# Two loads in another order, and a spacer of 32 bytes in place of 224, in a hybrid streaming encoder step

## The chip, the cores and the metric

The kernel runs on one core of one Trainium2 chip. The metric is the time of one execution on the device in microseconds, as the median of several executions. A profile of one more execution shows what each engine did: PE multiplies matrices (PEld is its loading of weights), DVE, ACT and POOL work on vectors, and SP issues the transfers (DMAs).

## What is computed

One step of a one-layer encoder for 1024 rows of a new stream and 16 new rows of each of 8 running streams, 1152 rows in all. Cut to its parts:

```python
def layer(h, p, past, mk, mv):
    mix, st = mixers(rmsnorm(h, p['norm_mix_g']), p, past)
    h = h + mix
    h = h + cross_attend(rmsnorm(h, p['norm_x_g']), mk, mv, p['wq_x'], p['wo_x'])
    h = h + swiglu(rmsnorm(h, p['norm_ffn_g']), p['w_gate'], p['w_up'], p['w_down'])
    return h, st
```

`mixers` runs three things side by side on the same normalised rows: a stick-breaking attention, a forgetting attention and a state-space mixer. The state-space mixer works in blocks of rows. For a block with channels x, B, C, step sizes dt and decays a, with `a_cum` the running sum of a over the block's rows:

```python
decay  = exp(where(causal, a_cum[t] - a_cum[s], -inf))
y      = ((C @ B.T) * decay) @ (x * dt) + (C @ h_in) * exp(a_cum)
h_out  = exp(a_cum[last]) * h_in + (B * exp(a_cum[last] - a_cum)).T @ (x * dt)
```

`swiglu` is `(silu(u @ w_gate) * (u @ w_up)) @ w_down` with 1024 inputs and 2816 hidden columns.

## The kernel before

All matrices are fp32. A product is made of three: each factor is split into a high part that PE multiplies at full rate and a low rest, and high x high, high x low and low x high are summed (`mm3`, line 340). PE is kept busy by many small generators that are interleaved in the text; a planner (line 2121, `schedule_with_timeline_sim=True`) then sets the order of instructions on each engine from the order of the text, the priorities (`tc.high_priority`) and a simulated time line. All transfers go through SP's one queue. SP issues in its order and stands still while one of its transfers waits for a tile to come free or for data to be written.

**The state-space blocks** (`ssd_gen`, line 979) run in nine blocks of 128 rows, the eight running streams first as block 8, then 0 to 7. They are interleaved with the forgetting attention of the new and the running streams. Before the first block the sums of all blocks are computed, transposed and stored to DRAM (`ac_sc`, line 1029). Then, for each block:

- `load` (line 1047) takes one `act` tile of 3072 floats a partition and fills it with three transfers: the block's convolved channels (`xbc_sc`, line 1049) into elements 0 to 1023, its running sums, one row of 1024 values sent to all partitions (`ac_sc`, line 1051), into 1024 to 2047, and its gate (`z_sc`, line 1053) into 2048 to 2559.
- `prepare` (line 1061) transposes the channels on PE (lines 1066 and 1070), copies them out on ACT (1067, 1071) and scales them on POOL (`heads_tt`, line 1042).
- `weights` (line 1076) multiplies C and B on PE (1081), masks on DVE (1083), and makes the decays from the running sums: differences on ACT (1089) and DVE (1091), the exponential on ACT (1094), the product on DVE (1097).
- `states` (line 1100) multiplies C with the state and B with x (1106, 1112) and updates the state on POOL and DVE; `outputs` (line 1164) multiplies the weights with x (1168), gates and normalises; `write` (line 1177) transposes the result (1180), copies it on ACT (1181) and stores it (1182).

The load of a block is requested one block ahead: after `prepare` of block n+1 the loop asks for block n+2 (line 1212). `prepare` of a block comes before its `weights` in the text.

**Gate and up** run in stage `gate_up` (line 1880). For each of 22 column blocks of the hidden layer, gate and up are taken together as a two-by-two block product with seven products in place of eight (a Winograd scheme): seven left factors made from the weights, and seven right factors made once from the normalised rows. The right factors are the tiles of `b_tiles` (line 1782), a high and a low tile for each of four sets, once with 256 columns (rows of blocks 0 to 3) and once with 320 (blocks 4 to 8). A product is twelve matmuls (four parts of the inner dimension, three splits each) at line 1918; the left factor is stationary and the right one moves. In the column blocks from 2 on, both widths alternate, twelve matmuls of one and then twelve of the other.

The pools on the left of the on-chip memory are stacked: constants, `raw` (2 x 4096 bytes a partition), `u` (3 x 5120), `tmp` (4640), `tl` (3 x 2304), then `gap`, one tile that nobody reads or writes, and then the right factors. When those are done, the last stage's pool `fin` (line 2009) begins where they began: the gain `gF`, the reloaded rows `h` and the outputs `y`. `LEAD` (line 34) is 8 floats, 32 bytes; it is also the distance by which `w_unit` (line 330) shifts split weights within their tiles for widths other than 512.

Of the kernel before, what the change touches and what calls it, by code (L numbers as in the profile page):

```python
# [8 lines left out]
F32 = mybir.dt.float32  # L9
# [8 lines left out]
P = 128  # L18
# [15 lines left out]
LEAD = 8  # L34
# [29 lines left out]
def tile_hybrid_step(ctx: ExitStack, tc: tile.TileContext, a: dict):  # L64
    nc = tc.nc
    ACT, DVE, POOL, PE, SP = nc.scalar, nc.vector, nc.gpsimd, nc.tensor, nc.sync
# [20 lines left out]
    def act_t(dt=F32R, home=None):  # L87
        return (home or actp).tile([P, 3072], dt, tag="act", name="act")

    def f_pool(name, bufs, side="left"):  # L90
        return tc.tile_pool(name=name, bufs=bufs, side=side, reuse_waits="tile")
# [55 lines left out]
    for k0 in (0, 2):  # L147
        first_raw.append(st_t(F32))
        SP.dma_start(out=first_raw[-1].rearrange("p (k n) -> p k n", n=512),
                     in_=a["wk_x"][0][k0 * P:(k0 + 2) * P, 0:512].rearrange("(k p) n -> p k n", p=P))  # L150
# [83 lines left out]
    def dram(shape, dt, name):  # L234
        return dr.tile(shape, dt, name=name, tag=name)
# [11 lines left out]
    ac_sc = dram([72, P], F32, "acsc")  # L247
# [731 lines left out]
    def ssd_gen():  # L979
# [66 lines left out]

        def load(i):
            A = act_t(F32)
            SP.dma_start(out=A[:, 0:1024].rearrange("p (j t) -> p j t", t=P),
                         in_=xbc_sc[:, i * P:(i + 1) * P].rearrange("(j p) t -> p j t", p=P))  # L1050
            SP.dma_start(out=A[:, 1024:2048],
                         in_=ac_sc[8 * i:8 * i + 8, :].rearrange("h t -> (h t)").unsqueeze(0).to_broadcast([P, 1024]))
            SP.dma_start(out=A[:, 2048:2560], in_=z_sc[i * P:(i + 1) * P, :])
            return A

        def views(A, B):
            xT = A[:, 0:1024].rearrange("p (j t) -> p j t", t=P)
            return (xT, A[:, 1024:2048], A[:, 2048:2560], B[:, 0:256], B[:, 256:512],
                    *(B[:, 512 + 512 * k:1024 + 512 * k] for k in range(4)))
# [124 lines left out]

        order, last = [8, 0, 1, 2, 3, 4, 5, 6, 7], None
        A, nxt = load(order[0]), None
        B = act_t(F32)
        st8 = [act_t(F32) for _ in range(2)]
        for b in range(8):
            SP.dma_start(out=st8[b // 4][:, 512 * (b % 4):512 * (b % 4 + 1)].rearrange("p (u n) -> p u n", n=P),  # L1190
                         in_=a["state_ssm"][0, b].rearrange("h p n -> (h p) n").rearrange("(u p) n -> p u n", p=P))
        prepare(order[0], A, B)
        yield
        weights(order[0], A, B)
        nxt = load(order[1])
        yield
        for n, i in enumerate(order):
            t1 = sg_t()
            yield from states(i, A, B, t1)
            yield  # L1200
            if i == 7:
                ps = pd()
                for j in range(4):
                    PE.transpose(ps[:, j * P:(j + 1) * P], hT[:, j * P:(j + 1) * P], ident)
                hn = sg_t()
                DVE.tensor_copy(hn, ps)
                SP.dma_start(out=a["p_ssm"][0, 0].rearrange("h p n -> (h p) n").rearrange("(j p) n -> p j n", p=P),
                             in_=hn.rearrange("p (j n) -> p j n", n=P))
            if n < 8:
                A1, B1 = nxt, act_t(F32)  # L1210
                prepare(order[n + 1], A1, B1)
                nxt = load(order[n + 2]) if n < 7 else None
                yield
            outputs(i, A, B, t1)
            yield
            if last:
                write(*last)
                yield
            last = (i, t1)
            if n == 8:  # L1220
                final.append(lambda: write(i, t1))
            if n < 8:
                weights(order[n + 1], A1, B1)
                yield
                A, B = A1, B1
# [62 lines left out]
    h = []  # L1288
# [381 lines left out]
    h = []  # L1670
# [49 lines left out]
    tmp = ctx.enter_context(f_pool("tmp", 1))  # L1720
    tlp = ctx.enter_context(f_pool("tlp", NL))
    gap = ctx.enter_context(f_pool("gap", 1))
    gap.tile([P, 56], F32, tag="gap", name="gap")
    bstack = ctx.enter_context(ExitStack())
    slots = [(tlp, "tl")]
    turn = [0]
# [398 lines left out]
```

## Time and profile before

| | us |
|---|---|
| median of 3 runs | 1865.63 |
| lowest and highest run | 1864.44 and 1869.66 |
| profiled execution, whole | 1863.43 |
| its span, first to last instruction | 1861.7 |
| mean granted clock of PE in it | 0.992 |

A line of the list of instructions or of the time line shows the start in us from the span's start, the duration in us, the engine, the source line, the operation, the tiles as out<-in, the shapes, and in brackets the idle time of the engine before it with what ended it. Matmuls overlap, so the distance of two starts, and not the duration, says how fast PE goes. A q behind an engine's name means its queue: SPq is SP issuing a transfer. The stages lie one behind another: memory keys and input projections to about 300 us, attention and state-space blocks to about 700, output projection and cross-attention to about 1080, gate and up from 1078.6 to 1583, the down projection and the final norm to the end.

### The profile page before, as it was taken

How to read it: one execution, taken by the hardware profiler on the slowest of the kernel's cores; microseconds unless marked ns; L12 is line 12 of the kernel's file. 1: busy time of each engine (PE TensorE's matmuls, PEld its weight loads, DVE VectorE, ACT ScalarE, POOL GpSimd, SP SyncE). 2: the span in 40 equal slices, each digit the busy share in tenths (PEclk: the TensorE clock that was granted, in tenths of full speed). 3: DMA queues.
4: the chain of work that ended last, by engine and by line, in shares of the span. 5: the costliest groups of instructions: out<-in, count | busy, mean ns of one | idle time of the engine just before them, and what ended most of it. 6: DMA issues, size and time to landing. Idle time of an engine off the chain costs nothing.

```text
span 1861.7 us, 32061 instructions
## 1 busy us (share of the span) xinstructions
PE 1804.3 (97%) x12008; PEld 1617.0 (87%) x12008; DVE 897.6 (48%) x1792; ACT 796.8 (43%) x1697; POOL 619.4 (33%) x921
## 2 busy tenths in 40 slices
PE   7999999999999999999999989999999999999998
PEld 5899878888966777899988889999999999888886
DVE  3412323476657864455553695333333334455554
ACT  6532544545456862343342564333333333344443
POOL 7622425445215663121021107444444542000000
PEclk9999999999999999999999989999999999999999
DMA  9465645437588883357873124322222223657572
GB/s 337 154 187 149 212 141 142 146 100 211 167 255 265 280 285 109 115 133 168 189 233 111 77 90 116 91 72 71 72 71 72 72 73 93 218 187 249 173 250 85
DMA packets 305547, 289.54 MB, mean 156 GB/s; under 512 B 113004, under 2 KB 257364, under 8 KB 305392
## 3 DMA queue, kind: packets, MB, share of 16 engines
q1 hardware_dynamic: 305392, 287.49, 50.7%
q8 instruction: 95, 1.56, 0.3%
q14 instruction: 60, 0.49, 0.1%
HBM read 221.58 MB, written 66.38 MB: 155 GB/s over the span
## 4 chain that ended last, share of the span: by engine, by line
PE 81%; DMA 6%; DVE 5%; POOL 3%; ACT 2%; issue 2%; SPq 1%; DVEq 0%; POOLq 0%; ACTq 0%
PE psd L1918 11%; PE psd L341 10%; PE psd L342 10%; PE psd L343 10%; PE pst L1918 8%; PE pss L1918 4%; PE pss L341 4%; PE pss L343 4%; PE pss L342 4%; PE pso L1918 2%; PE pst L343 2%; POOL wl L133 2%; PE pst L341 2%; PE pst L342 2%; PE pso L606 1%
## 5 line engine op out<-in xcount | busy, mean ns | idle before, releaser
L133 POOL TENSOR_TENSOR wl<-wr,wh 128x256 fp32r<-128x256 f32 (+2 forms) x152 | 121.2, 829 | 189.0 <-ACT wh L295 178.5
L341 PE MATMUL psd<-act,wh 128*128 128x384 f32 x528 | 182.1, 345 | 0.0
L343 PE MATMUL psd<-act,wl 128*128 128x384 f32 x528 | 180.0, 341 | 0.6 <-POOL wl L133 0.6
L342 PE MATMUL psd<-act,wh 128*128 128x384 f32 x528 | 179.5, 340 | 0.0
L1918 PE MATMUL pst<-bT,tr 128*128 128x256 f32 (+1 forms) x1068 | 155.1, 293 | 0.0
L1918 PEld LDWEIGHTS pst<-bT,tr 128*128 128x128 f32 x1068 | 144.9, 188 | 0.1
L342 PE MATMUL psd<-wl,act 128*128 128x256 f32 (+3 forms) x414 | 133.1, 322 | 2.5 <-POOL wl L133 2.4
L343 PE MATMUL psd<-wh,act 128*128 128x512 f32 (+3 forms) x424 | 135.3, 320 | 0.0
L341 PE MATMUL psd<-wh,act 128*128 128x256 f32 (+3 forms) x414 | 132.3, 323 | 1.8 <-ACT act L1397 1.4
L1918 PE MATMUL psd<-bT,tr 128*128 128x320 f32 (+1 forms) x912 | 132.9, 295 | 0.3 <-POOL tr L133 0.3
L1918 PEld LDWEIGHTS psd<-bT,tr 128*128 128x128 f32 x912 | 124.9, 188 | 0.6 <-POOL tr L133 0.6
L133 POOL TENSOR_TENSOR tr<-u,tr 128x256 fp32r<-128x256 f32 x110 | 82.7, 781 | 101.0 <-ACT tr L1754 83.1
L256 POOL TENSOR_SCALAR sm<-sm 128x1 f32<-128x1 f32 (+2 forms) x27 | 8.9, 330 | 294.7 <-ACT y L2029 206.9
L1893 DVE TENSOR_TENSOR tr<-tr,pst 128x256 f32<-128x256 f32 (+1 forms) x86 | 38.6, 449 | 139.9 <-ACT tr L1890 106.9
L343 PEld LDWEIGHTS psd<-act,wl 128*128 128x128 f32 x528 | 99.3, 188 | 3.1 <-issue 1.7
L133 POOL TENSOR_TENSOR ws<-ws 128x256 f32<-128x256 f32 (+2 forms) x100 | 69.4, 721 | 96.8 <-DVE ws L535 88.5
L341 PEld LDWEIGHTS psd<-act,wh 128*128 128x128 f32 x528 | 99.4, 188 | 2.4 <-issue 1.8
L342 PEld LDWEIGHTS psd<-act,wh 128*128 128x128 f32 x528 | 99.4, 188 | 1.8 <-issue 1.5
L133 POOL TENSOR_TENSOR tr<-raw,tr 128x256 fp32r<-128x256 f32 x94 | 69.3, 767 | 84.4 <-ACT tr L1754 76.2
L1754 ACT CAST tr<-u 128x512 fp32r<-128x512 f32 x130 | 76.7, 620 | 28.5 <-PE pst L1918 5.9
L342 PEld LDWEIGHTS psd<-wl,act 128*128 128x128 f32 x414 | 78.7, 190 | 10.0 <-POOL wl L133 4.3
L341 PEld LDWEIGHTS psd<-wh,act 128*128 128x128 f32 x414 | 78.8, 190 | 9.6 <-ACT act L1397 1.6
(645 smaller groups left out, 4635.4 us busy)
## 6 DMA issues: line engine op xcount, KB each, us to landing
u<-w_down SPq DMA_DIRECT2D x40, 512.0 KB
raw<-w_down SPq DMA_DIRECT2D x26, 512.0 KB
st<-qksc SPq DMA_DIRECT2D x48, 256.0 KB
wr<-w_in SPq DMA_DIRECT2D x44, 256.0 KB
tr<-hidsc SPq DMA_DIRECT2D x55, 192.0 KB
hidsc<-tr SPq DMA_DIRECT2D x34, 288.0 KB
qksc<-sg SPq DMA_DIRECT2D x48, 192.0 KB
wr<-cache_sb_k SPq DMA_DIRECT2D x32, 256.0 KB
```

Of the source, the lines that this page charges most:

```text
L133: POOL.tensor_tensor(out=out[:, a0:a1], in0=in0[:, a0:a1], in1=in1[:, a0:a1], op=op)
L256: POOL.tensor_scalar(v, ss, inv, EPS, ALU.mult, ALU.add)
L341: PE.matmul(out, ah, bh, start=start, stop=False)
L342: PE.matmul(out, ah, bl, start=False, stop=False)
L343: PE.matmul(out, al, bh, start=False, stop=stop)
L606: return PE.matmul(po[r:r + 64, q_], vt[:, 2 * (k0 + i) + j, :], pfs[i][:, sl], start=start and k0 == 0 and (j == 0 or qp > 0), stop=k0 + ...
L1754: ACT.copy(hi, src)
L1893: DVE.tensor_tensor(out=at(out, g), in0=at(x, g), in1=ps[g][:, :GW[g]], op=op)
L1918: PE.matmul(dst[g][:, :GW[g]], x[:, ka], y[:, k, :], start=start and k == 0 and m == 0, stop=stop and k == 3 and m == 2, skip_group_check= ...
```

## The change

In `load` of the state-space blocks the request for the running sums is moved ahead of the request for the channels. The two write different parts of the same tile. The `gap` tile shrinks from 56 floats to `LEAD`, 8 floats, which moves the right factors of gate and up, and later the tiles of `fin`, down by 192 bytes; counted in steps of 256 bytes they come to stand 64 bytes further on.

```diff
         def load(i):
             A = act_t(F32)
+            SP.dma_start(out=A[:, 1024:2048],
+                         in_=ac_sc[8 * i:8 * i + 8, :].rearrange("h t -> (h t)").unsqueeze(0).to_broadcast([P, 1024]))
             SP.dma_start(out=A[:, 0:1024].rearrange("p (j t) -> p j t", t=P),
                          in_=xbc_sc[:, i * P:(i + 1) * P].rearrange("(j p) t -> p j t", p=P))
-            SP.dma_start(out=A[:, 1024:2048],
-                         in_=ac_sc[8 * i:8 * i + 8, :].rearrange("h t -> (h t)").unsqueeze(0).to_broadcast([P, 1024]))
             SP.dma_start(out=A[:, 2048:2560], in_=z_sc[i * P:(i + 1) * P, :])
             return A
...
     gap = ctx.enter_context(f_pool("gap", 1))
-    gap.tile([P, 56], F32, tag="gap", name="gap")
+    gap.tile([P, LEAD], F32, tag="gap", name="gap")
```

## The prediction

> **What bounds the kernel now.** I read the page first, then two stages of the table of windows, then the chain and the waits of the stage that the first edit touches, and last the single matmuls of line 1918.
>
> ```profile
> span 1861.7 us, 32061 instructions
> PE 1804.3 (97%) x12008; PEld 1617.0 (87%) x12008; DVE 897.6 (48%) x1792; ACT 796.8 (43%) x1697; POOL 619.4 (33%) x921
> ```
>
> PE is busy for 97% of the span, so an edit pays if it shortens a matmul of a stage where PE never pauses, or if it takes away an idle moment of PE. There are only 57 us of those.
>
> ```profile
> 500.00:700.00 200.00, 187.67 (x1556) 144.43 (x1555) 131.41 (x379) 125.75 (x278) 99.42 (x165) 0.98 0.84 273
> 1200.00:1300.00 100.00, 100.00 (x756) 100.00 (x755) 36.09 (x63) 32.20 (x65) 47.70 (x64) 1.00 0.33 83
> ```
>
> The columns are the stretch, its length, busy time of PE, weight loads, DVE, ACT and POOL, granted clock, DMA share and GB/s. From 500 to 700 us the state-space blocks run: PE idles 12.3 us, and the DMA engines are 84% busy. At 1200 to 1300, gate/up, PE is busy throughout, every other engine is below half, and DMA stands at a third: there a nanosecond less per matmul is a nanosecond less of time.
>
> ```profile
> 510.26 9.17 DMA wr<-cache_fox_k
> 564.18 5.99 DMA s_ssm<-act
> 570.65 5.42 DMA act<-acsc
> 654.33 5.99 DMA act<-acsc
> ```
> ```profile
>   ACT act L1089: 11.0, 4
>   DVE act L1091: 8.7, 4
> ```
> ```profile
>   PE psd L1066: 1.7, 2
> ```
>
> The first fence holds the longest pieces of this stage's chain (start, length, what): it runs through loads of the running sums (acsc, line 1051). The other two say who waited for line 1051 and for the channels' load, line 1049 (us in total, times). ACT and DVE wait for the sums in four blocks each; PE itself waits only 1.7 us, for channels (xbcsc). A shorter ACT or DVE wait is worth only what it takes off PE's idle time.
>
> **The change: the order of two loads.** It adds and removes no instruction. In each of nine blocks SP asks for the sums where it asked for the channels, and for the channels next; the gate load stays third.
>
> ```profile
> 570.22 0.38 SPq L1049 DMA_DIRECT2D act<-xbcsc  x1
> ...
> 651.92 0.38 SPq L1049 DMA_DIRECT2D act<-xbcsc  x1
> 653.83 0.45 SPq L619 DMA_DIRECT2D mixsc<-so  x1
> 654.33 0.58 SPq L1051 DMA_DIRECT2D act<-acsc  x1
> ```
> ```profile
> 574.90 0.63 PE L1066 MATMUL psd<-identr,act 128*128 128x128 f32 x4 [1.42 <-DMA act<-xbcsc]
> ...
> 581.40 0.63 PE L1180 MATMUL psd<-identr,sg 128*128 128x128 f32 x4 [1.83 <-DVE sg L1175]
> ...
> 661.94 2.04 PE L1106 MATMUL psd<-act 128*128 128x256 f32 x4 [2.72 <-ACT sg L1181]
> ```
> ```profile
> 656.77 0.20 ACT L555 ACTIVATION_READ_ACCUMULATOR ws<-ws,sm 128x1 f32 x1
> 660.34 0.98 ACT L1089 ACTIVATE act<-act 128x128 f32<-128x128 f32 x3 [3.37 <-DMA act<-acsc]
> ```
>
> The bracket is the idle time before and what ended it. The largest idle moment of PE here, 2.72 us at 661.94, is made by this load: SP stood before a store (line 619) between the two requests, so the sums were asked for 2.41 us after the channels. ACT was free at 656.97, waited 3.37 us, did three pieces of line 1089, and only then the copy of line 1181 for which PE stood. With the sums at 651.92 they land about 2.4 us earlier, and PE's wait shrinks from 2.72 to about 0.3: **minus 2.4**. The store stays where it is; the channels of that block now go behind it, where PE did not wait for them.
>
> In an ordinary block the requests lie 0.43 us apart (570.22 and 570.65). There the channels had landed by 574.9 and the sums at 570.65 + 5.42 = 576.07: the second of the pair comes 1.2 us behind the first. Swapped, each load moves by up to that. DVE's wait ends 1.2 us sooner, and the chain takes that on to PE's 1.83 us at 581.40: **minus 1.2**. PE's own two waits for channels, 1.42 and 0.28 of the 1.7 us, grow to 2.6 and 1.5: **plus 2.4**. In the other blocks PE did not wait for channels. One of them could be brought to it, the block near 630, where SP is held 3.12 us in the second request:
>
> ```profile
> 630.02 3.12 SPq L1051 DMA_DIRECT2D act<-acsc  x1
> ```
>
> There the channels would be asked for 3 us later. I add nothing, at most one more such 1.2 us. The net is minus 1.2 us, with bounds of minus 3.6 (no PE wait grows) and plus 2.4 (the gain at 661.94 is lost to the next late thing, the block's other DMA loads at 84% DMA share).
>
> One more term could go with the 2.72 us:
>
> ```profile
> 576.00:583.00 7.00, 4.91 (x43) 4.70 (x43) 5.70 (x13) 4.89 (x12) 4.56 (x8) 1.00 1.04 407
> 661.94:668.09 6.15, 6.15 (x20) 5.22 (x21) 4.75 (x12) 4.46 (x10) 3.85 (x6) 0.50 0.64 219
> ```
>
> After this idle moment PE ran 6.15 us at half clock; around the 1.83 us one it kept 1.00. If the gap goes, up to half of 6.15, 3.1 us, goes too. I keep this for the range: the sum of several short gaps may do the same elsewhere.
>
> **The change: the right factors' place.** The pools ahead of B begin at byte 18112 in the kernel's layout; raw, u, tmp and tl take 8192, 15360, 4640 and 6912 bytes, gap 224. So every B tile begins at 53440, 192 past a multiple of 256; with a gap of 32 bytes, at a multiple of 256. All B sizes are multiples of 256, so each right factor moves alike. They are the moving operands of line 1918: 22 x 7 x 12 = 1848 products of 256 columns and as many of 320. The last pool (gF, h, y) moves too, off PE's path.
>
> ```profile
> 1114.52 1.58 PE L1918 MATMUL psd<-bT,tr 128*128 128x256 f32 x12
> ```
> ```profile
> 1252.50 3.35 PE L1918 MATMUL pss<-b,tr 128*128 128x256 f32 x24
> 1255.68 2.61 PE L1918 MATMUL psd<-bT,tr 128*128 128x256 f32 x19
> ```
> ```profile
> 129.73 0.28 PE L341 MATMUL psd<-wh,act 128*128 128x256 f32 x1
> ...
> 132.53 0.28 PE L341 MATMUL psd<-wh,act 128*128 128x256 f32 x1
> ...
> 1620.11 0.39 PE L341 MATMUL psd<-tl,tr 128*128 128x512 f32 x1
> ...
> 1622.83 0.39 PE L343 MATMUL psd<-tl,tr 128*128 128x512 f32 x1
> ```
>
> What counts is the distance from start to start. Twelve products of 256 columns take 1.58 us to the end of the last, which lasts 0.28 as in the rows of this width below: 1.30 / 11 = 118.2 ns. The 24 from 1252.50 to 1255.68 are twelve of each width, so a 320 takes (3.18 - 12 x 0.1182) / 12 = 146.8 ns. The projection of line 341 moves 256 columns too, out of weight tiles that begin 224 past a multiple of 256 and are read 32 bytes on (LEAD), at a multiple. From 129.73 to 132.53 lie 24 of them: 116.7 ns. **The same width costs 1.5 ns less there: 1848 x 1.5 = 2.8 us.**
>
> For 320 columns no row shows a start at a multiple. 512 columns starting at 224 take 2.72 / 12 = 226.7, so a column costs (226.7 - 146.8) / 192 = 0.416 ns. Above that stand 10.2 ns for 256 at 0, 11.7 for 256 at 192, and 13.7 for 320 at 192 and 512 at 224. Two readings fit: the excess grows with the width (then 320 gains nothing), or with the start's distance past the multiple (then 13.7 falls to about 10.2, 3.5 ns). I take the gain of the nearest row, 1.5 ns, again **2.8 us**; bounds are 0 and 13.7 x 1848 = 25 us. No row gives a reason for a loss; below nothing I take the same 1.5 ns.
>
> [...]
>
> **The sum.** 1.2 + 2.8 + 2.8 = 6.8 us off. The profiled execution took 1863.43 us, 1.7 of it outside the span; it would take 1856.6. The median of the three runs, 1865.63, lies 2.2 higher, so I forecast 1858.8.
>
> **Rivals.** (1) *The place is worth nothing*: the 1.5 ns belong to the other matmul stream (other weights, another destination), not to the start. Only the loads remain, minus 1.2: 1864.4; with the half clock too, 1861.3. Against it: width and kind of operand are the same. [...] (2) *The start explains all the excess*: 320 gains 3.5 ns, 6.5 us, and the half clock goes: 1.2 + 2.8 + 6.5 + 3.1 = 13.6, so 1852.0. (3) *Channels come late and PE cools*: its wait at 574.90 grows to 2.6 us, close to the 2.72 that stood before the half clock at 661.94. Half clock there costs 3.1 us, and if ACT at 661 is held by another load the 2.4 are not won: 2.4 - 1.2 + 3.1 - 5.6 = minus 1.3: 1864.3. It decides at which idle length PE cools, by the rows between 1.83 and 2.72 us. [...] (4) *Slower: SP is held in the first block.*
>
> ```profile
> 509.34 0.37 SPq L1049 DMA_DIRECT2D act<-xbcsc  x1
> ...
> 536.47 0.32 SPq L1051 DMA_DIRECT2D act<-acsc  x1
> ```
>
> The first block's sums can be read only after line 1029 has stored them. If the planner puts line 1051 where 1049 stood, SP waits from 509.34 to 536.47, and the cache load that the chain has at 510.26 stands behind it: up to 27 us, less what other work PE has. I take 20 and the matmuls' gain of 5.6 off: 1880. It decides if the written order is kept against readiness; against it, SP now puts line 1190's loads, which come later in the text, ahead of line 1051.
>
> **Chances.** Forecast 0.45 (1855 to 1862), (1) 0.15, (2) 0.15, (3) 0.17, (4) 0.08. A measurement tells about 0.3%, 5.6 us, from no change: below 1860.0 faster, above 1871.2 slower. Faster: 0.32 + 0.02 + 0.14 + 0.02 = 0.50. Slower: (4) and 0.02 of the rest, 0.10. Same: 0.40. The range 1850 to 1868 leaves out (4), the 25 us bound and the tails.
>
> **What would show it.** The 256-wide starts of line 1918 at 116.7 ns; the 320-wide at 145.3 (146.8 kills that half, 143.3 is rival 2). At the last block's load line 1051 ahead of the store, PE's wait before line 1106 under 0.5 us (a half clock that is gone there would be 3.1 us beyond the forecast); the waits before line 1066 at about 2.6 and 1.5. I am wrong if 256 columns stay at 118, or if PE's idle time from 500 to 700 is not below 12.3 us.

## The result and the profile after

| | before | after |
|---|---|---|
| median, us (five runs of each, on one chip) | 1867.28 | 1879.23 |
| lowest and highest run | 1864.44 and 1871.27 | 1874.83 and 1883.36 |
| profiled execution, whole | 1863.43 | 1882.01 |
| its span | 1861.7 | 1880.3 |

The ratio is 1.0061, with a 95% interval of 1.0035 to 1.0087: the changed kernel is 11 us slower, the interval 7 to 16. The forecast was 1858.8, with a range that ended at 1868 and a chance of 0.1 for slower. It was wrong, and in its sign.

The head of the page after, and the two stretches of the table of windows that the prediction showed of before (stretch, length, busy time of PE, weight loads, DVE, ACT, POOL, granted clock, DMA share, GB/s):

```profile
span 1880.3 us, 32061 instructions
...
PE 1810.9 (96%) x12008; PEld 1620.5 (86%) x12008; DVE 896.4 (48%) x1792; ACT 796.6 (42%) x1697; POOL 618.1 (33%) x921
```
```profile
500.00:700.00 200.00, 185.06 (x1458) 142.07 (x1457) 128.37 (x383) 121.04 (x273) 94.39 (x161) 0.94 0.83 260
1200.00:1300.00 100.00, 100.00 (x758) 100.00 (x757) 37.55 (x65) 33.75 (x68) 44.65 (x60) 1.00 0.31 77
561.24:581.72 20.48, 19.25 (x70) 11.87 (x71) 9.73 (x33) 8.83 (x18) 1.89 (x3) 0.50 0.70 189
```

The instructions are the same ones, 32061 of them, and gate/up is as full as before. The loss is in the first row: between 500 and 700 us PE idles 14.9 us where it idled 12.3, and its granted clock is 0.94 where it was 0.98, which over 200 us is 8 us more. The third row holds most of that: 20.5 us in one piece at half clock, with PE busy in 94% of it. Idle time and clock of this row make 10.6 us, about the measured loss. (The profiled pair lies further apart, 18.6 us. From 700 to 750 PE idles 2.3 us more, and before 500 us, 4.1 us more. A later run with the changed kernel's order of the loads has 0.4 of those 4.1, so they belong mostly to that one execution.)

The waits of PE from 500 to 720 us after (who waited for what, us in total, times, longest):

```profile
PE pst L591 <- DVE ws L560: 3.1, 3, 1.3
...
PE psd L1151 <- DVE act L1156: 1.6, 1, 1.6
PE pst L1141 <- DMA act<-state_ssm: 1.6, 1, 1.6
...
PE psd L1066 <- DMA act<-xbcsc: 0.3, 1, 0.3
PE psd L1106 <- ACT sg L1181: 0.2, 1, 0.2
```

The wait that the change was aimed at is gone: 0.2 us before line 1106 in place of 2.7. The wait that I feared, for channels at line 1066, did not grow but fell from 1.7 to 0.3. In their place stand waits that before did not have, among them one for the *states* (`state_ssm`, line 1190), which the diff does not touch. SP's queue says why. First before, then after (in the changed kernel line 1049 is the sums and line 1051 the channels):

```profile
512.54 2.63 SPq L1190 DMA_DIRECT2D act<-state_ssm  x2
...
524.98 4.55 SPq L1190 DMA_DIRECT2D act<-state_ssm  x4
...
532.91 0.35 SPq L1029 DMA_DIRECT2D acsc<-so  x1
```
```profile
516.26 0.55 SPq L1051 DMA_DIRECT2D act<-xbcsc  x1
...
535.83 0.33 SPq L1029 DMA_DIRECT2D acsc<-so  x1
...
537.64 0.40 SPq L1049 DMA_DIRECT2D act<-acsc  x1
538.10 1.15 SPq L1190 DMA_DIRECT2D act<-state_ssm  x2
...
540.04 5.69 SPq L1190 DMA_DIRECT2D act<-state_ssm  x6
```

Before, the planner put all eight state loads ahead of the first block's sums, in the time in which SP would have stood for them. After, it leaves the channels where they were and puts all eight behind the sums, the first of them 25 us later. PE feels it at once (time line of PE after):

```profile
543.35 0.66 PE L1141 MATMUL pst<-identr,act 128*128 128x128 f32 x4 [1.61 <-DMA act<-state_ssm]
...
562.48 1.19 PE L1151 MATMUL psd<-act 32*128 32x256 f32 x2 [1.62 <-DVE act L1156]
```

At the second of these gaps the long stretch at half clock begins. And SP is only one queue: the planner made another order for all five engines. Listed by source line and tile in the order of their starts in the traces, 543 of PE's 12008 matmuls and 138 of DVE's 1792 instructions stand elsewhere than before; in a kernel of the changed spacer alone, none does.

### The profile page after: what moved, and what is told of

Read it like the earlier page. It is cut to its first block, busy times and chain, and to the rows that moved or that the text cites. A ratio compares the mean times of both kernels' runs of the same rounds, so it can differ in the third digit from the quotient of the medians.

```text
span 1880.3 us, 32061 instructions
## 1 busy us (share of the span) xinstructions
PE 1810.9 (96%) x12008; PEld 1620.5 (86%) x12008; DVE 896.4 (48%) x1792; ACT 796.6 (42%) x1697; POOL 618.1 (33%) x921
## 4 chain that ended last, share of the span: by engine, by line
PE 82%; DMA 7%; DVE 4%; POOL 3%; ACT 2%; issue 2%; SPq 1%; DVEq 0%; POOLq 0%; ACTq 0%
PE psd L1918 11%; PE psd L341 9%; PE psd L342 9%; PE psd L343 9%; PE pst L1918 8%; PE pss L341 4%; PE pss L1918 4%; PE pss L343 4%; PE pss L342 4%; PE pso L1918 2%; PE pso L606 2%; PE pst L343 2%; PE pst L342 2%; PE pst L341 2%; POOL wl L133 1%
```

## Experiments

Five theories ran through them. **A**: the late state loads of the first block make the loss. **B**: the place of the right factors makes it. **C**: both edits take part. **D**: channels that come late in the other blocks make it. **E**: before is one good plan among many, and any other plan of this stage is slower, whatever the edit that led to it. The table has all runs but two, which come at the end; PE's idle time and granted clock are those of one profiled execution from 500 to 740 us (240 less its busy time, and the clock's column of the table of windows), so that the clock counts 2.4 us for a hundredth. For e1 the profiled execution was its fastest (1872.1 us, the others 1879.8 to 1883.2), for e9 its slowest (1892.1, the others 1872.7 to 1883.8), so these two rows are no mean of their kernels.

| run | what differs from before | ratio to before (95%) | idle, us | clock |
|---|---|---|---|---|
| before | | 1 | 14.0 | 0.99 |
| after | both edits | 1.0061 (1.0035 to 1.0087) | 18.9 | 0.95 |
| e1_loads | loads, all blocks | 1.0066 (1.0047 to 1.0085) | 19.6 | 0.99 |
| e2_place | spacer | 0.9984 (0.9968 to 1.0000) | 12.0 | 0.99 |
| e3_not_first | loads, blocks 0 to 7 | 1.0044 (1.0027 to 1.0061) | 19.3 | 0.99 |
| e4_first_only | loads, first block | 1.0108 (1.0083 to 1.0132) | 22.3 | 0.91 |
| e5_last_only | loads, last block | 0.9998 (0.9977 to 1.0019) | 14.2 | 1.00 |
| e7_states_ahead | loads, all; states first | 1.0030 (1.0012 to 1.0049) | 19.9 | 0.96 |
| e8_states_ahead_old_order | states first | 1.0086 (1.0052 to 1.0120) | 24.0 | 0.94 |
| e9_channels_third | sums, gate, channels | 1.0051 (1.0028 to 1.0074) | 24.1 | 0.92 |
| n5_priority | a priority 101 for 100 | 1.0076 (1.0060 to 1.0092) | 22.3 | 0.95 |
| n2_gate_block3 | gate first, block 3 | 1.0021 (1.0008 to 1.0034) | 21.0 | 0.98 |
| n6_priority99 | a priority 99 for 100 | 1.0009 (0.9988 to 1.0029) | 13.6 | 0.99 |
| n7_priority104 | a priority 104 for 100 | 1.0108 (1.0069 to 1.0147) | 25.7 | 0.94 |
| n9_priority110 | a priority 110 for 100 | 1.0063 (1.0043 to 1.0083) | 20.4 | 0.96 |

Each execution's granted clock over the whole span is on record as well. Its median is 0.990 or 0.991 for before and 0.991 or 0.992 for e2, e5 and n6, but 0.986 for after and 0.984 to 0.987 for e1, e4, e7, e8, n5, n7 and n9. As PE is busy nearly all the time, half a hundredth of 1870 us is about 9 us: by this estimate most of after's loss is PE at half clock, and the idle moments themselves are the smaller part. e3, e9 and n2, at 0.990, lose mostly by other things than the clock.

### Which edit

The loads alone, and the spacer alone:

```diff
-            SP.dma_start(out=A[:, 0:1024]..., in_=xbc_sc...)
             SP.dma_start(out=A[:, 1024:2048], in_=ac_sc...)
+            SP.dma_start(out=A[:, 0:1024]..., in_=xbc_sc...)
```


> Only the order of the two loads is changed; the spacer stays at 224 bytes. Theory A (the loss is made in the first state-space block: once the sums' request stands ahead in the text, the planner puts the eight state loads of line 1190 behind it, at 538 us instead of 512, and the whole stage starts late): the time of the changed kernel, 11 us over before (ratio about 1.006), the first line 1168 near 582 instead of 565, and PE at half clock somewhere in 540 to 600. Theory B (the place of the right factors costs the time): no more than 2 us from before. Theory C (both edits carry part): between 3 and 8 us.

```diff
-    gap.tile([P, 56], F32, tag="gap", name="gap")
+    gap.tile([P, LEAD], F32, tag="gap", name="gap")
```


> Only the spacer is changed, so the order of the work is that of before. Theory A: within 2 us of before, the 256-wide starts of line 1918 at 117 to 118 ns and the 320-wide at 147. My prediction's terms would make it 5.6 us faster (116.7 and 145.3 ns). Theory B: 8 to 11 us slower, with line 1918's stage longer than 504.5 us.

The loads alone give the whole loss: 1.0066. The spacer alone gives 0.9984, which is 3 us off with an interval from 6 to 0. B and C fall. The waits of PE from 500 to 760 us with the loads alone:

```profile
PE pst L1141 <- DMA act<-state_ssm: 2.7, 2, 2.2
PE pst L591 <- DVE ws L560: 2.6, 3, 1.0
PE pst L900 <- DMA wr<-cache_fox_k: 2.4, 3, 1.4
PE psd L1151 <- DVE act L1156: 1.7, 1, 1.7
```

These are the waits of after again. But the profiled execution had only 3.4 us at half clock at this place, where after has 20.5. It took 1872.1 us at a granted clock of 0.992; the other five of this kernel took 1879.8 to 1883.2 at 0.984 to 0.987. So PE lost more to the half clock in these five. They have no trace, and that they lost it at this place is likely but not shown.

### Which block

The condition is `i < 8` in e3, `i == 8` in e4 and `i == 7` in e5.

```diff
+            for o in (1, 0) if i < 8 else (0, 1):
+                SP.dma_start(out=(channels, sums)[o], in_=(xbc_sc..., ac_sc...)[o])
```


> The sums go first in blocks 0 to 7, but not in the first block (number 8); spacer as before. The eight state loads then stand where before has them. Theory A: no loss; 0 to 5 us faster than before (the prediction's 1.2 for the loads, up to 3.1 if the half clock near 662 goes). Theory D (channels that come late in the later blocks make the loss): 8 to 11 us slower. Theory E (any other plan of this stage moves the time by several us, up or down, wherever the swap is): somewhere from 8 faster to 10 slower, with no tie to the state loads.

> The sums go first in the first block alone; spacer as before. Theory A: all of the loss, 9 to 15 us slower than before, the state loads at 538, the first line 1168 near 582. Theory D: no change within 3 us.

A foretold e4, which lost even more, and failed at e3: without the first block's swap, with the state loads where they had been, the kernel is still 8 us slower. The parts do not add: 8 and 20 us alone, 12 together. That is the first sign of E. For D spoke that PE did wait in e3 at line 1066 (time line of PE):

```profile
580.13 0.63 PE L1066 MATMUL psd<-identr,act 128*128 128x128 f32 x4 [1.07 <-DMA act<-xbcsc]
...
609.78 0.63 PE L1066 MATMUL psd<-identr,act 128*128 128x128 f32 x4 [1.22 <-DMA act<-xbcsc]
...
708.66 1.11 PE L1180 MATMUL psd<-identr,sg 128*128 128x128 f32 x4 [3.59 <-DVE st L1334]
```

But these two waits, 2.3 us, are hardly more than the 1.7 of before, and the largest gap, 3.59 us where before has 1.7, was ended by line 1334, which belongs to the output projection.

> The sums go first only in the last block (number 7), the one where my prediction saw 2.4 us at PE's 2.72 us gap and up to 3.1 us of half clock behind it; spacer as before. If that step was right by itself: the gap before line 1106 under 0.5 us, and 2 to 5 us faster than before (ratio 0.997 to 0.999). If the planner fills the moment with another wait (theory E: each new plan of this stage is paid for elsewhere): within 2 us of before, or slower.

This is the prediction's main step by itself, and the nearest to an edit of the loads with the rest held still: 48 of PE's matmuls stand elsewhere than before. Its gap before line 1106 is gone, the half clock behind it too (clock 1.00), and no gain was measured: 0.9998, with an interval of 4 us to either side. PE's time line shows what is late next:

```profile
669.41 0.30 PE L591 MATMUL pst<-identr,ws 128*128 128x128 f32 x1 [1.93 <-DVE sm L260]
```

The gap has moved from the state-space block to the attention beside it. A rule of "minus 2.4 where the wait was 2.7" takes the next waiter to be ready; it was 1.9 us away.

### Loads later or earlier

```diff
-        A, nxt = load(order[0]), None
+        A, nxt = act_t(F32), None
         B = act_t(F32)
         st8 = [act_t(F32) for _ in range(2)]
         for b in range(8):
             SP.dma_start(out=st8[b // 4]..., in_=a["state_ssm"][0, b]...)
+        load(order[0], A)
```


> The sums go first in all nine blocks as in the changed kernel, and the eight state loads of line 1190 are asked for ahead of the first block's load; spacer as before. Theory A (late state loads are the larger part of the loss with all nine blocks swapped): PE no longer waits for them before line 1141 (2.7 us in the run with the loads alone), no long half clock near 560, and the time falls to that of the swap without the first block, about 8 us over before, or below. If they are not the cause: 12 us over before, as with the loads alone.

> The channels go first as before, and the eight state loads are asked for ahead of the first block's load: it sets the run above apart from the mere effect of earlier state loads. If the order of channels and sums costs something by itself, this is several us faster than the run above and within 3 us of before. Theory E (before is a plan picked among many, and any other plan of this stage costs some us): also 5 to 10 us slower than before, although no load of it comes later than needed.

With the sums first, putting the states ahead brings 1.0066 down to 1.0030 (the two intervals just touch), and PE waits for states no more: A had probably seen a real part. But A had also foretold that no long half clock would stand near 560, and 10.2 us of it begin at 552.6. With the channels first, as before, the same edit costs 16 us. A did not expect that. Nor are channels first the better order here: with the states ahead, sums first is the faster of the two. In both kernels the first block's channels go out behind the states, so they are no control without a later load; the priorities below are.

```diff
+            for o in (1, 2, 0) if i < 8 else (0, 1, 2):
+                SP.dma_start(out=(channels, sums, gate)[o], in_=(xbc_sc..., ac_sc..., z_sc...)[o])
```


> In blocks 0 to 7 the order is sums, gate, channels, so that the channels come still later than in the run with sums first in these blocks (8 us over before); first block and spacer as before. Theory D (late channels make the loss of the later blocks): more than 8 us slower than before, PE's waits before line 1066 for channels above the 2.3 us of that run. Theory E: anything from 3 to 12 us slower, with no longer waits for channels.

From PE's waits in e3, and then in e9:

```profile
PE psd L1066 <- DMA act<-xbcsc: 2.3, 2, 1.2
```
```profile
PE psd L1066 <- DMA act<-xbcsc: 4.5, 2, 2.5
```

The wait for channels doubled, as D said, though in e9's slowest execution. The ratios, 1.0051 against 1.0044, have intervals that overlap, so 2.2 us more could hide in them. But in e3 PE waits for channels only 0.6 us longer than in before, so D can carry a small part of its 8 us at most.

### Other plans with the loads as they were

```diff
-HP = {"av": 100, "xa": 100}
+HP = {"av": 101, "xa": 100}
```


> Loads and spacer as before; one planner priority (HP, for the attention's products) is 101 instead of 100. No transfer is asked for in another order for a reason of data, and the state loads and the first block's channels keep their place ahead of the sums; only the planner makes another plan of the same work. Theory E (before is a plan picked among many, so another plan of the state-space stage costs some us by itself): 3 to 12 us slower than before. Theories A and D (the loss is made by the late state loads and the late channels alone): within 2 us of before.

And, with HP at 100 again:

```diff
+            if i == 3: gate()
             channels, sums
-            gate()
+            if i != 3: gate()
```


> Spacer and the order of channels and sums as before; in block 3 alone the gate, which is used last, is asked for first. By the work of its transfer it moves channels and sums of one block some 0.5 us later. Theory E: 3 to 12 us slower than before, from the new plan. Theory D: within 2 us.

`HP` ranks the attention's products for the planner. One step of it, with every load in the text as before, makes the kernel 14 us slower, more than the change did. PE's time line of that run:

```profile
550.57 0.69 PE L968 MATMUL pst<-fold,so 128*128 128x64 f32 x2 [2.75 <-DVE so L964]
...
585.88 1.29 PE L900 MATMUL pst<-identr,wr 128*128 128x128 f32 x8 [4.09 <-DMA wr<-cache_fox_k]
...
674.23 0.30 PE L900 MATMUL pst<-identr,wr 128*128 128x128 f32 x1 [2.84 <-ACT sg L1181]
...
716.23 0.66 PE L1180 MATMUL psd<-identr,sg 128*128 128x128 f32 x4 [3.42 <-DVE st L1334]
```

Other lines wait, for other things, with the same outcome: more idle time (22.3 us) and a lower granted clock (0.95) in the same stretch. The gate of one block, moved ahead of the two other loads, costs 4 us, and with it 142 of PE's matmuls stand elsewhere than before. One such plan could be a mishap, so three more followed:

> Loads and spacer as before; the attention's priority HP is 99 instead of 100. The plan of SP, VectorE and GpSimd is that of before, and TensorE's differs in 113 lines of an earlier stage alone. Theory E (the loss comes with another plan of the state-space stage): within 3 us of before. If a plan's time hangs on anything at all: 3 us or more away.

> Loads and spacer as before; HP is 104. The planner makes another order of all engines from about 500 us on, with no transfer changed. Theory E: 3 to 15 us slower than before, in PE's idle time and half clock between 500 and 740 us. If the one plan with 101 (14 us slower) was a single mishap: on either side of before, as likely faster as slower.

> Loads and spacer as before; HP is 110, a third plan of the same work. Theory E: 3 to 15 us slower than before. If 101 was a single mishap: on either side of before.

99 leaves the state-space stage as it was (10 of PE's matmuls stand elsewhere, all of them before 475 us) and takes the time of before. 104 and 110 plan it anew and are 20 and 12 us slower. In the traces of 101, 104 and 110 the state loads are asked for ahead of the first block's sums, from 508 to 516 us on; PE waits for no state and for channels 0.5 to 0.9 us, less than the 1.7 of before. So neither A nor D makes these losses. (With the gate of block 3 first, PE waits 3.7 us for channels, so D may have a part in those 4 us.) That is E, as the table has it in one column: in the kernels that are no slower than by 0.1% (before, e2, e5, n6) PE idles 12.0 to 14.2 us; in all the others, where 142 to 543 of PE's matmuls stand elsewhere, it idles 18.9 to 25.7.

### The place of the factors

```diff
-    gap.tile([P, 56], F32, tag="gap", name="gap")
+    gap.tile([P, 58], F32, tag="gap", name="gap")
```


> Loads as before; the spacer is 232 bytes, so that the right factors begin 200 bytes past a multiple of 256 and no longer at a multiple of 16. If a start counts only by its distance from a multiple of 256 (my reading, small as it proved): line 1918's 256-wide starts at 122.4 ns in the mean, as at 192, and the stage at 504.5 us. [...]

The last run joins the spacer of e2 and the loads of e5:

> The two parts of the change that did no harm alone: sums first in the last block only, and the spacer of 32 bytes. If they add (0.9984 and 0.9998 alone): 2 to 5 us faster than before, ratio about 0.998.

The time lines of line 1918, with the spacer alone (start at a multiple of 256), then with 232 bytes (start 200 past one), and then in the joined run (a multiple of 256 again):

```profile
1253.48 3.33 PE L1918 MATMUL psd<-bT,tr 128*128 128x256 f32 x24
...
1259.83 3.33 PE L1918 MATMUL psd<-bT,tr 128*128 128x256 f32 x24
1263.00 1.57 PE L1918 MATMUL pst<-bT,tr 128*128 128x256 f32 x12
1264.41 1.92 PE L1918 MATMUL pso<-bT,tr 128*128 128x320 f32 x12
1266.17 3.34 PE L1918 MATMUL pst<-bT,tr 128*128 128x256 f32 x24
```
```profile
1253.45 3.36 PE L1918 MATMUL psd<-bT,tr 128*128 128x256 f32 x24
...
1259.86 3.36 PE L1918 MATMUL psd<-bT,tr 128*128 128x256 f32 x24
1263.06 1.60 PE L1918 MATMUL pst<-bT,tr 128*128 128x256 f32 x12
1264.49 1.93 PE L1918 MATMUL pso<-bT,tr 128*128 128x320 f32 x12
1266.26 3.36 PE L1918 MATMUL pst<-bT,tr 128*128 128x256 f32 x24
```
```profile
1266.90 1.56 PE L1918 MATMUL pst<-bT,tr 128*128 128x256 f32 x12
1268.30 1.92 PE L1918 MATMUL pso<-bT,tr 128*128 128x320 f32 x12
1270.06 3.32 PE L1918 MATMUL pst<-bT,tr 128*128 128x256 f32 x24
```

With the spacer alone, twelve products of 256 columns take 1264.41 - 1263.00 = 1.41 us, 117.5 ns each, and twelve of 320 take 1.76, 146.7 ns each. At 200 they take 119.2 and 147.5. Two rows of 24 take 6.35 us with the spacer alone, 6.41 at 200, and 6.36 before (3.18 twice). By these rows the move from 192 is worth 0.005 us a row, and there are 154 rows: 0.8 us. The counts of the table of windows agree: from 1200 to 1575 us PE starts 2840 of these products before, 2845 with the spacer alone and 2823 with 232 bytes, 0.2% more and 0.6% fewer, or 0.9 us off and 3 us on over the stage's 504. (The run with 232 bytes is a single execution, of 1863.1 us in all.) In that execution the start at 200 cost 1.7 ns at 256 columns and 0.8 ns at 320 over the start at a multiple of 256, more than the move from 192 brought.

The joined run does not fit this. Its right factors stand where those of e2 stand, yet twelve products of 256 columns take 1.40 us, 116.7 ns each, as the prediction had it; those of 320 stay at 146.7. It starts 2858 products in the same windows, 0.6% more than before, about 3 us of the stage. So the start does not fix this time by itself, and what else does stays open. The whole came out at 0.9991 (0.9976 to 1.0007): no version was shown to beat before.

## Why the prediction was wrong, step by step

- **"It adds and removes no instruction"** and the sum built on it. This step failed. True as it stands, it was used as if nothing else moved: each of the three terms (minus 2.4, minus 1.2, plus 2.4) was read from the waits of before's plan. The edit changes the input of the planner that orders all five engines, and the waits of that plan are not in the new one. Five of five other plans of the whole stage without the swap of sums and channels (e8, n2, n5, n7, n9) were slower, by 4 to 20 us. The swap's plan, at 12, is one of this kind.
- **Minus 2.4 at line 1106.** The wait went, as foretold (0.2 us after), but not in the foretold way: the store did not stay between the two requests, both now stand behind it (670.29 and 670.73 us in SP's time line). Done alone (e5) it gave no gain that could be measured: the attention's line 591 waited 1.9 us instead, and PE's idle time was 14.2 us against 14.0.
- **Minus 1.2, and plus 2.4 at line 1066.** Neither can be found. The wait of 1.83 us before line 1180 is not in the new plan, and the waits for channels fell to 0.3.
- **Idle time from 500 to 700 below 12.3 us.** It is 14.9. The prediction named this row as the one that would show it wrong.
- **The half clock, "for the range".** The sign was wrong. It went at 662, and 20.5 us of it came at 561. The clause that several short gaps may do the same elsewhere was a guess with no price in the sum: in after, gaps of 1.61 and 1.62 us stand near the starts of its two pieces of half clock, but that they made them was not shown.
- **256 columns at 116.7 ns, 320 at 145.3.** Mis-sized: 117.5 and 146.7 with the spacer alone. The second is the number that the prediction named as killing its half, so that half was nothing. The first was worth about 0.7 ns x 1848 = 1.3 us in place of 2.8; the joined run did reach 116.7, so the term was possible, but the start was not enough for it. Rival 1 was near in its size here. That line 341's 116.7 ns belong to another matmul stream was not tested. In all, the move from 192 to a multiple of 256 brought about 1 us of the 5.6 forecast (3 us in the joined run), and the start at 200 lost about 3 us in its one execution (e6).
- **Rival 4, SP held in the first block.** The nearest, at a chance of 0.08. The sums' request was indeed the one that matters, but the channels kept their place and the cache loads did not stand behind it; the state loads did. The rows were on hand: the prediction itself noted that line 1190's loads, later in the text, went ahead of line 1051, and did not ask what would keep them there.

What stays open: why the planner let the state loads pass the sums in one text and not in the other, and how much of the 12 us is the state loads' own. e7 puts it near 7, the difference of 1.0066 and 1.0030, but the two intervals allow 2 to 12, and e7 is another plan as well.

## What to carry to other kernels

Where a planner orders the engines from the text, an edit's first cost is a new plan, and the waits of the old profile say little about it; the old plan, if it was the best of several, will mostly be better than the next. Hold the plan still (few lines of difference in order) before reading a gain from a wait, and run one or two edits without meaning, such as a priority moved by one step, to learn how far the time strays by itself. A gap that is taken away is worth its length less the distance to the next late thing, and here that left nothing that could be measured.

## What the runs showed of the chip

From 500 to 740 us PE's half clock (0.50 in the table of windows) came in pieces of 3.4 us or multiples: 6.8 in before at 661, 3.4 at 544 and 20.5 at 561 after. A gap of 1.61 us ended 0.8 us before the second of these, and the third began in a gap of 1.62. In before a gap of 1.83 was harmless (granted clock 1.00 from 576 to 583 us), and the prediction put the limit between that and 2.72; in e5 one of 1.93 was harmless too (1.00 from 650 to 700). So in these traces no single idle length decides. The 20.5 us began only 0.4 us into their gap (560.86 to 562.48), after 3.4 us in which PE was busy for 3.0.

In the 20.5 us PE was busy 94% of the time and still did not get its clock back, with transposes (line 1141 and others) and products of few rows or columns (lines 1144 and 1151); before, 6.15 us in which PE never paused sufficed (granted clock 0.50 to 668.09 us, 1.00 from there to 671). The longest pieces of five other kernels begin in the same work of the first block, 17.1 us in e4, e9 and n5, 13.7 in n9 and 10.2 in e7. In e4 (first row of windows) PE was busy for all of its 17.1 us at half clock; before (second row) did that work at full clock with PE busy for 22.2 us of 24.4:

```profile
558.55:575.62 17.07, 17.07 (x66) 10.31 (x63) 6.92 (x22) 8.13 (x17) 3.37 (x6) 0.50 0.82 227
```
```profile
538.40:562.80 24.40, 22.20 (x186) 13.87 (x185) 18.80 (x71) 13.01 (x29) 0.80 (x2) 1.00 0.74 206
```

What in this work costs the clock was not tested.

Nor was the clock the same in every execution of one kernel: e1's took 1872.1 us once, at a granted clock of 0.992, and 1879.8 to 1883.2 us five times, at 0.984 to 0.987.
